# One transfer per attention unit for queries, keys and results, and a fixed order of conv taps and attention steps

## The chip, the core and the metric

The kernel runs on one core of a Trainium2 chip. The metric is the time of one execution on the device in microseconds (us), read as the median of several runs. The core has a matmul engine (TensorE, PE in the profile, with its weight loads as PEld), a vector engine (VectorE, DVE), an engine for activations and copies (ScalarE, ACT), a general engine (GpSimd, POOL) and a queue (SyncE, SP) that here issues every DMA.

## The reference

One hybrid decoder block over 2048 positions and 1024 channels, in float32. A normalized input is projected into eight sections. One branch is a gated depthwise convolution with 31 taps, a layer norm, SiLU and a gate; the other is sliding-window attention with 16 query heads, 4 key/value heads of 64 and a sink for each head. Both are projected out, merged by per-channel sigmoid gates, projected again and added to the input, and the sum is normalized.

```
h = rmsnorm(x); glu_in, conv_gate, q, k, v, attn_gate, merge = split(h @ w_in)
c = a * sigmoid(b)                    # a, b = halves of glu_in
c = silu(layernorm(depthwise_conv(c, 31 taps, causal) + b_dw))
y_conv = (c * silu(conv_gate)) @ w_conv_out
s = rope(q) . rope(k) / 8             # queries in blocks of 128, keys: own and previous block
s = where(0 <= distance < 128, s, -1e30); m = max(max(s), sink)
p = exp(s - m); probs = p / (sum(p) + exp(sink - m))
y_attn = ((probs @ v) * silu(attn_gate)) @ w_attn_out
out = rmsnorm(x + (g_conv * y_conv + g_attn * y_attn) @ w_out)
```

## The kernel before

**Precision.** Each float32 operand of a product is split into a high half (a cast) and a low half (the difference), and each product is three matmuls: high by high, low by high, high by low. Names with `whi_` and `wlo_` are the halves of a weight; `raw_` is the weight as it is loaded, in two transfers of 128 x 512 (0 and 1 at the end of a name). ScalarE casts it (L268) and GpSimd subtracts (L253). The low half is stored to `d_lo` in the first sweep (L284) and loaded from there in the second (L270).

**Sweeps and items.** The sequence is done in two sweeps of 1024 positions. In each, TensorE works through a list of items; an item is one 128-column slice of a projection over two halves of 512 positions, 16 products, each of three matmuls of 128 x 512 in a planned time of 0.68 us. The items of the projections are named ga/gb (the convolution's input), q_a/q_b, v, ag (attention gate), cg (conv gate), ma/mc (merge gates); later come ya, yc and o. TensorE's order is the program's.

**Conv taps.** VectorE does the convolution: eight groups of 128 channels, 31 taps each, one instruction of 128 x 1024 per tap (L513 for the first, L520 for the others), 248 in a sweep. The program emits one for every 2.4 us of planned time while attention runs.

**Attention.** A sweep has 32 units (4 key/value heads by 8 blocks of 128 queries), one for every 13.8 us of planned time. Queries and keys are stored to DRAM in split halves (`d_q`, L648; `d_k`), and each unit loads its own: four query transfers (L736) and four key transfers (L740) of 32 partitions each into a tile `qk`. Values are stored to `d_v`, and `load_v` (L715) brings them back for four blocks of one head in six transfers into `vm`, `va`, `vb`. A unit's steps are: scores `sc` on TensorE (L774) into two PSUM banks; ScalarE copies (L787, L789) and VectorE's masked copies (L790) into `ss`; the maximum on VectorE (L793, `st`); four exponentials on ScalarE (L795); the reciprocal (L797); four scalings on ScalarE (L799); four transposes on TensorE (L804, `tpp`); the cast on ScalarE (L813) and the split on VectorE (L253 from L814) into `pt`; two masked parts on GpSimd (L817, `pc`); the product with the values (L828, `ov`); two copies, two sums, the gate and a split (L836 to L842), and two transfers of the result to `d_a`. `sc` (twice), `tpp` and `ov` take turns on three PSUM banks, so the second bank of a unit's scores is the one that the split of the unit before sets free.

**What sets the order.** `Line` plans a time: each product adds 0.68 us to it, and a generator's step that is due is emitted between two products (`yield a, b`: TensorE time that the step costs, and how long until the next step). So steps stand in the program, and on TensorE, by planned time. On the other engines and on the queue a scheduler orders instructions by priority and planned readiness; a `Line` step and what stands in `front()` has a high priority. A conv tap may so be placed well ahead of its place in the program, or between two steps of one unit. `prepare_attention` flushes the stores of queries, loads unit 0's queries and keys, and twelve transfers of values.

## Time and profile before

| | |
|---|---|
| median of 3 runs | 2027.77 us |
| lowest and highest run | 2024.05, 2028.27 us |
| profiled execution | 2025.42 us |
| its span | 2023.7 us |
| mean granted TensorE clock | 0.995 |
| DMA packets, bytes | 302784, 382.03 MB |

One execution was profiled. Its span runs from the first to the last instruction that the page counts, 1.7 us less than the time of that execution. Times in the views are microseconds from the start of the span. In a group, `xN` is the number of instructions, followed by busy time, mean duration in ns, and the engine's idle time just before them with the instruction that ended it. In a timeline a row is start, duration, engine, line, operation, result and source, with the idle time before it in brackets. `SPq` is the queue that issues DMAs: the duration there is that of the issue, not of the transfer. Attention runs from about 197 to 690 us in the first sweep, and from about 1194 to 1684 us in the second.

### The profile page before, as it was taken

Reading aid. Unit: us, or ns where it says so; the run is one execution under the profiler, and the core shown is the slowest. Engines: PE = TensorE matmul, PEld = TensorE weight load, DVE = VectorE, ACT = ScalarE, POOL = GpSimd, SP = SyncE. Lnnn points to the kernel's source line nnn. Section 1 sums busy time; section 2 is a strip of 40 time slices with the busy share of each in tenths; the row PEclk is TensorE's granted clock in tenths of the full one; section 3 lists DMA queues with packets and bytes.
Section 4 is the critical chain, followed back from the end, with each engine's and each line's share of the span. In section 5 each row is a group of like instructions: output and inputs, shape, how many; then the busy total and the mean of one; then the engine's idle time right before and its main releaser. Section 6 shows DMA issues by size and latency. Waiting matters only on the chain.

```text
span 2023.7 us, 27913 instructions
## 1 busy us (share of the span) xinstructions
PE 1989.0 (98%) x9264; PEld 1656.4 (82%) x9264; DVE 1302.1 (64%) x1737; ACT 976.3 (48%) x2253; POOL 430.2 (21%) x462
## 2 busy tenths in 40 slices
PE   8999999999999999999999999999999999999998
PEld 7888788888888888888887887888888888888887
DVE  7999569878984275143857668579878834431424
ACT  7322576555546356244523125765565554552422
POOL 0444233333323322340011121111111110001200
PEclk9999999999999999999999999999999999999999
DMA  8655655556566855356646556665666677554532
GB/s 304 207 168 175 218 173 187 181 178 186 177 195 212 272 191 190 118 197 236 216 151 210 157 162 204 180 186 176 182 180 192 192 234 253 190 174 136 200 128 83
DMA packets 302784, 382.03 MB, mean 189 GB/s; under 512 B 30000, under 2 KB 160944, under 8 KB 302640
## 3 DMA queue, kind: packets, MB, share of 16 engines
q1 hardware_dynamic: 302640, 380.25, 58.0%
q8 instruction: 73, 1.20, 0.2%
q14 instruction: 71, 0.58, 0.1%
HBM read 252.20 MB, written 127.93 MB: 188 GB/s over the span
## 4 chain that ended last, share of the span: by engine, by line
PE 64%; DVE 16%; ACT 5%; issue 4%; DMA 1%; POOL 0%; SPq 0%; ACTq 0%; DVEq 0%; POOLq 0%
DVE acc L520 10%; PE mm_mc L291 9%; PE o L1148 9%; PE mm_ya L291 9%; PE mm_yc L291 9%; PE mm_ma L291 6%; PE mm_ag L291 5%; PE mm_ga L291 5%; PE mm_gb L291 4%; PE mm_q_a L291 2%; PE mm_q_b L291 2%; PE sc L774 1%; ACT ss L795 1%; DVE st L793 1%; PE mm_v L291 1%
## 5 line engine op out<-in xcount | busy, mean ns | idle before, releaser
L520 DVE SCALAR_TENSOR_TENSOR acc<-glu,par,acc 128x1024 f32<-128x1024 f32 x464 | 595.6, 1284 | 6.3
L1148 PE MATMUL o<-wo,mT 128*128 128x512 f32 x768 | 174.8, 389 | 0.0
L1148 PEld LDWEIGHTS o<-wo,mT 128*128 128x128 f32 x768 | 144.2, 188 | 30.0
L291 PE MATMUL mm_ag<-hT,whi_ag 128*128 128x512 f32 x512 | 161.0, 396 | 0.0
L291 PE MATMUL mm_cg<-hT,whi_cg 128*128 128x512 f32 x512 | 160.1, 394 | 0.0
L291 PE MATMUL mm_ma<-hT,whi_ma 128*128 128x512 f32 x512 | 160.0, 394 | 0.0
L795 ACT ACTIVATE ss<-ss,st 128x129 f32<-128x129 f32 x256 | 100.2, 394 | 123.9 <-DVE st L793 123.6
L291 PE MATMUL mm_mc<-hT,whi_mc 128*128 128x512 f32 x512 | 158.3, 390 | 0.0
L291 PE MATMUL mm_ya<-aT,whi_ya 128*128 128x512 f32 x512 | 157.7, 389 | 0.0
L291 PE MATMUL mm_yc<-uT,whi_yc 128*128 128x512 f32 x512 | 157.7, 389 | 0.0
L817 POOL TENSOR_SCALAR_AFFINE_SELECT pc<-pt 64x512 fp32r<-64x512 f32 x128 | 83.6, 653 | 311.1 <-ACT pt L813 268.8
L291 PE MATMUL mm_ga<-hT,whi_ga 128*128 128x512 f32 x448 | 141.4, 397 | 0.0
L291 PE MATMUL mm_gb<-hT,whi_gb 128*128 128x512 f32 x448 | 140.7, 395 | 0.6 <-DVE rb_q__1_1660 L602 0.6
L291 PEld LDWEIGHTS mm_ya<-aT,whi_ya 128*128 128x128 f32 x512 | 96.1, 188 | 20.0
L291 PEld LDWEIGHTS mm_yc<-uT,whi_yc 128*128 128x128 f32 x512 | 96.1, 188 | 19.9
L291 PEld LDWEIGHTS mm_mc<-hT,whi_mc 128*128 128x128 f32 x512 | 95.4, 188 | 19.4
L291 PEld LDWEIGHTS mm_ag<-hT,whi_ag 128*128 128x128 f32 x512 | 94.2, 190 | 17.8
L291 PEld LDWEIGHTS mm_ma<-hT,whi_ma 128*128 128x128 f32 x512 | 93.1, 188 | 17.2
L291 PEld LDWEIGHTS mm_cg<-hT,whi_cg 128*128 128x128 f32 x512 | 92.9, 188 | 17.0
L291 PE MATMUL mm_ag<-hT,wlo_ag 128*128 128x512 f32 x256 | 100.6, 393 | 3.6 <-DMA wlo_ag<-d_lo 3.6
L291 PE MATMUL mm_cg<-hT,wlo_cg 128*128 128x512 f32 x256 | 100.0, 391 | 0.0
L291 PE MATMUL mm_ma<-hT,wlo_ma 128*128 128x512 f32 x256 | 100.0, 391 | 0.0
(450 smaller groups left out, 4218.1 us busy)
## 6 DMA issues: line engine op xcount, KB each, us to landing
qk<-d_q SPq DMA_DIRECT2D x256, 64.0 KB, 2.6
d_a<-ss SPq DMA_DIRECT2D x128, 128.0 KB, 2.6
aT<-d_a SPq DMA_DIRECT2D x32, 512.0 KB, 5.3
qk<-d_k SPq DMA_DIRECT2D x240, 64.0 KB, 2.0
d_q<-hq_c SPq DMA_DIRECT2D x16, 512.0 KB, 4.2
raw_ag<-in_w_in_dram SPq DMA_DIRECT2D x32, 256.0 KB, 3.4
d_ag<-ag SPq DMA_DIRECT2D x32, 256.0 KB, 2.5
pc<-d_ag SPq DMA_DIRECT2D x64, 128.0 KB, 2.5
```

The lines of the kernel that those rows point to most:

```text
L291: pe.matmul(out=ps, lhsT=a, rhs=b, start=(k == 0 and i == 0), stop=(k == KC - 1 and i == 2))
L520: dve.scalar_tensor_tensor(out=to, in0=glu[c][:, j:j + T], scalar=tap(c, j), in1=acc[c], op0=ALU.mult, op1=ALU.add)
L774: pe.matmul(out=scs[qh][:, hp, c0:3 * HD], lhsT=w, rhs=k[:, j, qh * HD + c0:qh * HD + 3 * HD], start=(j == 0), stop=(j == 1))
L793: dve.tensor_reduce(out=ngm, in_=ext, axis=AX.X, op=ALU.max, negate=True)
L795: act.activation(out=ext[:, h, :], in_=ext[:, h, :], func=AF.Exp, bias=ngm[:, h:h + 1], accum_out=den[:, h:h + 1])
L817: pool.affine_select(out=pc[at], in_=f(pt[0:HD, a]), pattern=[[0, 2 * GQ], [1, HD]], compare_op=ALU.is_ge, fill=0.0, base=0, channel_multi ...
L1148: pe.matmul(out=ps, lhsT=a[:, c0:c0 + P], rhs=r, start=(k == 0 and i == 0), stop=(k == KC - 1 and i == 2))
```

## The change

*Layouts and transfers.* `d_q`, `d_k` and `d_a` get layouts in which a unit's data are one block: one transfer for its queries (128 x 512), one for its keys (128 x 512, or 128 x 256 in the first block), and one for its result, in place of four, four and two. Keys are stored with high and low half beside each other, in two transfers per call in place of one. Scores read the keys in pieces of 64 columns with the other half between them.

*Order.* A function `od` puts a mark "chain" on an instruction; marked ones keep the program's order among each other on their engine. It is put on the conv taps, on attention's steps on VectorE and ScalarE, and on the loads of weights, values, queries and keys. `front()` is no longer used there.

*Pieces.* The generator of a unit yields more often, so its steps are emitted in more and smaller pieces, each with its own planned time. A set `soft` is now what tells whether a unit of that head has come so far that the next head's attention gate must have been stored.

```diff
@@ -156,10 +156,10 @@
...
-    d_q = dram.tile([2, 2, P, S // HD, 2, P], F32, name="d_q")
-    d_k = dram.tile([2, 2, P, S], F32, name="d_k")
-    d_a = dram.tile([NSWEEP * KC, P, 2, T], F32, name="d_a")
+    d_q = dram.tile([P, 2, 2, S // HD, 2, P], F32, name="d_q")
+    d_k = dram.tile([P, 2, 2, S // HD, 2, HD], F32, name="d_k")
+    d_a = dram.tile([NSWEEP * NKV, P, 2, 2, T], F32, name="d_a")
     d_v = dram.tile([S // P, P, 2, NKV, P], F32, name="d_v")
...
+    def od(op):
+        tc.stamp_issue_order_token(op.ins, "chain")
+        return op
     n_w = 84
...
                 raw, hi, lo = (home[i][:, kh] for i in range(3))
-            nc.sync.dma_start(out=raw, in_=src[:, 4 * kh:4 * kh + 4, :])
+            od(nc.sync.dma_start(out=raw, in_=src[:, 4 * kh:4 * kh + 4, :]))
             act.copy(hi, raw)
             if (at, kh) in lo_stored:
-                nc.sync.dma_start(out=f(lo), in_=d_lo[at, kh])
+                od(nc.sync.dma_start(out=f(lo), in_=d_lo[at, kh]))
             else:
...
                 acc[c] = cv_ps.tile([P, T], F32, tag="acc", name=f"acc{s}_{c}")
-                dve.tensor_scalar(out=acc[c], in0=glu[c][:, 0:T], scalar1=tap(c, 0), scalar2=cbias(c),
-                                  op0=ALU.mult, op1=ALU.add)
+                od(dve.tensor_scalar(out=acc[c], in0=glu[c][:, 0:T], scalar1=tap(c, 0), scalar2=cbias(c),
+                                     op0=ALU.mult, op1=ALU.add))
...
                     to = cv[c] = slot(C[c], [P, T], F32, f"cv{s}_{c}")
-                dve.scalar_tensor_tensor(out=to, in0=glu[c][:, j:j + T], scalar=tap(c, j),
-                                         in1=acc[c], op0=ALU.mult, op1=ALU.add)
+                od(dve.scalar_tensor_tensor(out=to, in0=glu[c][:, j:j + T], scalar=tap(c, j),
+                                            in1=acc[c], op0=ALU.mult, op1=ALU.add))
                 if j == TAPS - 1:
...
         def store_k(i, half, src):
-            hl = slot(next_of("hl", AT[7:11]), [P, 2, TH], F32R, f"hlk{s}_{half}_{i}")
-            put_split(hl, src, dve)
-            t0 = s * T + half * TH
-            nc.sync.dma_start(out=d_k[:, i, :, t0:t0 + TH].rearrange("a p t -> p a t"), in_=f(hl))
+            hl = slot(next_of("hl", AT[7:11]), [P, NB, 2, HD], F32R, f"hlk{s}_{half}_{i}")
+            src = src.rearrange("p (b t) -> p b t", t=HD)
+            act.copy(hl[:, :, 0], src)
+            split_lo(hl[:, :, 1], src, hl[:, :, 0], dve)
+            b0 = 2 * s * NB + half * NB
+            for a in range(2):
+                nc.sync.dma_start(out=d_k[:, a, i, b0:b0 + NB], in_=f(hl))
...
             def load(to, rows, kind, blk):
-                nc.sync.dma_start(out=f(to), in_=d_v[blk, rows, kind, g].rearrange("b p d -> p b d"))
+                od(nc.sync.dma_start(out=f(to), in_=d_v[blk, rows, kind, g].rearrange("b p d -> p b d")))
...
             t = slot(next_of("qk", AT[11:13]), [P, 2, 4 * P], F32R, f"qk{s}_{n}")
-            q, k = t[:, 0, :].rearrange("p (b t) -> p b t", t=P), t[:, 1, :].rearrange("p (a t) -> p a t", a=2)
+            q, k = t[:, 0, :].rearrange("p (b t) -> p b t", t=P), t[:, 1, :].rearrange("p (b a t) -> p b a t", a=2, t=HD)
             qk[n] = (q, k)
             fs = slice(g * HH, (g + 1) * HH)
-            for i in range(4):
-                nc.sync.dma_start(out=f(q[i * HH:(i + 1) * HH]), in_=d_q[i // 2, i % 2, fs, 2 * blk:2 * blk + 2].rearrange("p b h t -> p (b h) t"))
-            k0 = max(blk - 1, 0) * P
-            nk = (blk + 1) * P - k0
-            for i in range(4):
-                nc.sync.dma_start(out=f(k[i * HH:(i + 1) * HH, :, 2 * P - nk:]),
-                                  in_=d_k[:, i % 2, fs, k0:k0 + nk].rearrange("a p t -> p a t"))
-        begun = set()
+            od(nc.sync.dma_start(out=f(q), in_=d_q[fs, :, :, 2 * blk:2 * blk + 2].rearrange("p a i b h t -> (p a i) (b h) t")))
+            b0 = 2 * max(blk - 1, 0)
+            nb = 2 * blk + 2 - b0
+            od(nc.sync.dma_start(out=f(k[:, 4 - nb:]), in_=d_k[fs, :, :, b0:b0 + nb].rearrange("p a i b c t -> (p a i) b c t")))
+        begun, soft = set(), set()
...
                         pe.matmul(out=scs[qh][:, hp, c0:3 * HD], lhsT=w,
-                                  rhs=k[:, j, qh * HD + c0:qh * HD + 3 * HD], start=(j == 0), stop=(j == 1))
+                                  rhs=k[:, qh + c0 // HD:qh + 3, j, :], start=(j == 0), stop=(j == 1))
...
                 pool.memset(sb, NEG)
-            with front():
-                for qh, sc in enumerate(scs):
-                    part = sb[:, 2 * qh:2 * qh + 2, :]
-                    if not first:
-                        act.copy(part, sc[:, :, 0:P])
-                    elif qh:
-                        act.copy(part[:, :, HD:], sc[:, :, HD:P])
-                    dve.copy_predicated(out=part[:, :, 0:HD], mask=tri_i, data=sc[:, :, P:3 * HD])
+            parts = [sb[:, 2 * qh:2 * qh + 2, :] for qh in range(2)]
+            for qh, part in enumerate(parts):
+                if not first:
+                    od(act.copy(part, scs[qh][:, :, 0:P]))
+                elif qh:
+                    od(act.copy(part[:, :, HD:], scs[qh][:, :, HD:P]))
+            yield 0.90, 0.8
+            for part, sc in zip(parts, scs):
+                od(dve.copy_predicated(out=part[:, :, 0:HD], mask=tri_i, data=sc[:, :, P:3 * HD]))
             st = work.tile([P, 3, GQ], F32, tag="st", name=f"st{u}", bufs=4)
             ngm, den, rinv = (st[:, i, :] for i in range(3))
-            dve.tensor_reduce(out=ngm, in_=ext, axis=AX.X, op=ALU.max, negate=True)
+            od(dve.tensor_reduce(out=ngm, in_=ext, axis=AX.X, op=ALU.max, negate=True))
+            yield 0.0, 1.2
             for h in range(GQ):
-                act.activation(out=ext[:, h, :], in_=ext[:, h, :], func=AF.Exp, bias=ngm[:, h:h + 1],
-                               accum_out=den[:, h:h + 1])
-            dve.reciprocal(out=rinv, in_=den)
+                od(act.activation(out=ext[:, h, :], in_=ext[:, h, :], func=AF.Exp, bias=ngm[:, h:h + 1],
+                                  accum_out=den[:, h:h + 1]))
+            yield 0.0, 3.3
+            od(dve.reciprocal(out=rinv, in_=den))
+            yield 0.0, 0.6
             for h in range(GQ):
-                act.activation(out=sb[:, h, :], in_=sb[:, h, :], func=AF.Copy, scale=rinv[:, h:h + 1])
-            yield 0.90, LAT[0]
+                od(act.activation(out=sb[:, h, :], in_=sb[:, h, :], func=AF.Copy, scale=rinv[:, h:h + 1]))
+            soft.add(n)
+            yield 0.0, LAT[0] - 5.9
...
             flat = tpp.rearrange("p h q -> p (h q)")
-            with front():
-                act.copy(pt[:, 0], flat)
-                split_lo(pt[:, 1], flat, pt[:, 0], dve)
+            od(act.copy(pt[:, 0], flat))
+            yield 0.44, 0.5
+            od(split_lo(pt[:, 1], flat, pt[:, 0], dve))
             for a in range(2):
...
                                    compare_op=ALU.is_ge, fill=0.0, base=0, channel_multiplier=-1)
-            yield 0.44, LAT[1]
+            yield 0.0, LAT[1] - 0.5
...
             to = [oT[own].rearrange("p i (q t) -> p i q t", t=HD) for own, _ in rows]
-            with front():
-                for r in range(2):
-                    act.copy(to[r], ovp[rows[r][1], :, r])
-                for r in range(2):
-                    dve.tensor_tensor(out=to[r], in0=ovp[rows[r][0], :, r], in1=to[r], op=ALU.add)
-            dve.tensor_tensor(out=oT, in0=oT, in1=ga, op=ALU.mult)
+            for r in range(2):
+                od(act.copy(to[r], ovp[rows[r][1], :, r]))
+            yield 0.72, 0.6
+            for r in range(2):
+                od(dve.tensor_tensor(out=to[r], in0=ovp[rows[r][0], :, r], in1=to[r], op=ALU.add))
+            od(dve.tensor_tensor(out=oT, in0=oT, in1=ga, op=ALU.mult))
+            yield 0.0, 1.6
             hl = sb.rearrange("p (l c) q -> p l c q", c=2)
-            act.copy(hl[:, 0].bitcast(F32R), oT)
-            split_lo(hl[:, 1].bitcast(F32R), oT, hl[:, 0], dve)
+            od(act.copy(hl[:, 0].bitcast(F32R), oT))
+            yield 0.0, 0.5
+            od(split_lo(hl[:, 1].bitcast(F32R), oT, hl[:, 0], dve))
             if n == NKV * NB - 1 and s + 1 < NSWEEP:
...
                     "p g (a d) -> p g a d", d=HD))
-            yield 0.72, 4.0
+            yield 0.0, 1.0
...
             def store():
-                for i in range(2):
-                    nc.sync.dma_start(out=d_a[e2, :, i, qs].rearrange("c p q -> p c q"), in_=hl[:, i])
+                nc.sync.dma_start(out=d_a[s * NKV + g, :, :, :, qs], in_=hl)
                 done[n] = True
...
                 line.after(22.0 + n * ATT_EVERY, attention(n),
-                           lambda n=n: (n > 0 or 0 in qk or 0 in begun) and (n not in begun or ("ag", 2 * (n // NB) + 1) in stored))
+                           lambda n=n: (n > 0 or 0 in qk or 0 in begun) and (n not in soft or ("ag", 2 * (n // NB) + 1) in stored))
             line.every = CONV_EVERY
...
```

Line numbers after the change are 5 to 11 higher: taps L518 and L525 for L513 and L520, masked copies L796 for L790, maximum L799 for L793, reciprocal L805 for L797, the split L258 for L253, loads L272 and L275 for L267 and L270, L723 for L715, L743 and L746 for L736 and L740.

The orders below show instructions as they stand on an engine, each with the line, the operation, the result and the source (numbers at the end of a name tell buffers apart).

VectorE, first sweep, fifth block of the second head (`ss_1_4`, with the split `pt_1_3` of the block before), and `acc`, the tap that is added. Before:

```order
L790 COPY_PREDICATED ss_1_4_3591<-tri,sc_1_4_0_3581 128x2x64
L520 SCALAR_TENSOR_TENSOR acc_4_3628<-glu_4_3225,par,acc_4_3628 128x1024
L790 COPY_PREDICATED ss_1_4_3591<-tri,sc_1_4_1_3586 128x2x64
L520 SCALAR_TENSOR_TENSOR acc_4_3628<-glu_4_3225,par,acc_4_3628 128x1024
L793 TENSOR_REDUCE st_1_4_3597<-ss_1_4_3591 128x4
L520 SCALAR_TENSOR_TENSOR acc_4_3628<-glu_4_3225,par,acc_4_3628 128x1024 x2
L797 RECIPROCAL st_1_4_3597<-st_1_4_3597 128x4
L520 SCALAR_TENSOR_TENSOR acc_4_3628<-glu_4_3225,par,acc_4_3628 128x1024
L253 TENSOR_TENSOR pt_1_3_3650<-tpp_1_3_3643,pt_1_3_3650 128x512
```

After the change, the same place:

```order
L796 COPY_PREDICATED ss_1_4_3501<-tri,sc_1_4_0_3491 128x2x64
L796 COPY_PREDICATED ss_1_4_3501<-tri,sc_1_4_1_3496 128x2x64
L799 TENSOR_REDUCE st_1_4_3517<-ss_1_4_3501 128x4
L518 TENSOR_SCALAR acc_4_3533<-glu_4_3139,par 128x1024
L525 SCALAR_TENSOR_TENSOR acc_4_3533<-glu_4_3139,par,acc_4_3533 128x1024
L805 RECIPROCAL st_1_4_3517<-st_1_4_3517 128x4
L525 SCALAR_TENSOR_TENSOR acc_4_3533<-glu_4_3139,par,acc_4_3533 128x1024
L258 TENSOR_TENSOR pt_1_3_3564<-tpp_1_3_3557,pt_1_3_3564 128x512
```

Both masked copies and the maximum now follow each other, and three taps stand ahead of the split in place of five. The first tap of group 4 (L518) stands here now, and before further up.

The queue (SP), second sweep, the weights of the second q_b item: `wlo_q_b` is the low half of its second transfer, `d_v<-vt` and `d_v<-vd` stores of values. Before:

```order
L687 DMA d_v<-vd_1_1_9893 128x4x256
L685 DMA d_v<-vt_2_9781 128x2x256
L685 DMA d_v<-vt_3_9785 128x2x256
L715 DMA vb_10726<-d_v 64x4x128 x2
L715 DMA va_10725<-d_v 64x4x128
L715 DMA vb_10726<-d_v 64x4x128
L270 DMA wlo_q_b_9823<-d_lo 128x512
```

After the change:

```order
L272 DMA raw_q_b_9605<-in_w_in_dram 128x512
L695 DMA d_v<-vd_0_1_9562 128x4x256
L693 DMA d_v<-vt_2_9565 128x2x256
L693 DMA d_v<-vt_3_9569 128x2x256
L275 DMA wlo_q_b_9607<-d_lo 128x512
L272 DMA raw_gb_10_9712<-in_w_in_dram 128x512
```

No load of values stands ahead of the weights any more, and the low half comes right behind the stores of the first pair of values.

The queue, first sweep, where attention begins: `raw_ga_20` and `raw_ga_21` are the weights of the ga item beside which the first scores stand. Before:

```order
L267 DMA raw_ga_20_1777<-in_w_in_dram 128x512
L284 DMA d_lo<-wlo_ag_01_1592 128x512
L267 DMA raw_ga_21_1783<-in_w_in_dram 128x512
L740 DMA qk_0_1745<-d_k 32x2x128 x4
L648 DMA d_q<-hq_2_0_a_1461 128x8x128
L648 DMA d_q<-hq_2_0_c_1462 128x8x128
L648 DMA d_q<-hq_2_2_a_1465 128x8x128
L736 DMA qk_0_1745<-d_q 32x512
```

After the change:

```order
L723 DMA va_1753<-d_v 64x4x128
L723 DMA vb_1754<-d_v 64x4x128
L573 DMA d_ag<-ag_0_0_1716 128x512
L656 DMA d_q<-hq_2_1_a_1505 128x8x128
L656 DMA d_q<-hq_2_1_c_1506 128x8x128
L573 DMA d_ag<-ag_0_1_1771 128x512
L272 DMA raw_ga_20_1775<-in_w_in_dram 128x512
L272 DMA raw_ga_21_1781<-in_w_in_dram 128x512
```

The two weight loads stood ahead of the first queries and keys; now they stand behind them, behind twelve loads of values and four stores.

More of the change, by code (lines that the diff above doesn't have):

```diff
@@ L252, in split_lo @@
     def split_lo(out_, full, hi, eng):
-        eng.tensor_tensor(out=out_, in0=full, in1=f(hi), op=ALU.subtract)
+        return eng.tensor_tensor(out=out_, in0=full, in1=f(hi), op=ALU.subtract)
     def load_w(src, name, home=None, steps=None):
@@ L648, in store @@
                         pend.append(lambda a=a: nc.sync.dma_start(
-                            out=d_q[a, i, :, b0:b0 + NB, r // 2, :],
+                            out=d_q[:, a, i, b0:b0 + NB, r // 2, :],
                             in_=f(pair[n][a]).rearrange("p b h t -> p b (h t)")))
@@ L939, in a_op @@
             aT[h][e] = slot(AT[8 * h + e], [P, 2, TH], F32R, f"aT{s}_{h}_{e}")
-            nc.sync.dma_start(out=f(aT[h][e]), in_=d_a[s * KC + e, :, :, h * TH:(h + 1) * TH])
+            nc.sync.dma_start(out=f(aT[h][e]), in_=d_a[s * NKV + e // 2, :, :, e % 2, h * TH:(h + 1) * TH])
         a_ops = [lambda e=e, h=h: a_op(e, h) for h in range(2) for e in range(KC)]
```

## The prediction

> **What bounds the kernel now.** I read the page's head and busy lines first, then the waits of TensorE, then the stretches around each wait, and last the timeline of the engines that end them.
>
> ```profile
> span 2023.7 us, 27913 instructions
> PE 1989.0 (98%) x9264; PEld 1656.4 (82%) x9264; DVE 1302.1 (64%) x1737; ACT 976.3 (48%) x2253; POOL 430.2 (21%) x462
> ```
>
> TensorE is busy for 1989.0 of 2023.7 us, and the change leaves it the same matmuls. So the most that can be won is TensorE's idle time, 34.7 us, and some hidden in its busy time as a slow clock. The waits view (line, releaser: us, times, longest) says where the idle time is:
>
> ```profile
> PE sc L774 <- DVE pt L253: 10.4, 13, 1.6
> PE mm_gb L291 <- ACT u_c L361: 5.5, 1, 5.5
> PE mm_q_b L291 <- DMA wlo_q_b<-d_lo: 4.4, 1, 4.4
> PE mm_ag L291 <- DMA wlo_ag<-d_lo: 3.6, 1, 3.6
> PE sc L774 <- issue: 2.9, 1, 2.9
> PEld sc L774 <- DVE pt L253: 13.3, 16, 1.8
> ```
>
> Five causes. The 5.5 us at mm_gb is the start of the program, which the change doesn't touch. The others it does: score matmuls (sc) that wait for VectorE's pt split, in 16 places by the weight loads' count; two places that wait for a weight's low half; and the first scores, which wait for queries. The view by windows (PE, PEld, DVE, ACT, POOL busy, then the granted clock, DMA share, GB/s) shows what a stop costs beside itself:
>
> ```profile
> 413.00:416.00 3.00, 3.00 (x8) 2.32 (x8) 2.92 (x5) 0.45 (x1) 1.28 (x1) 0.51 0.75 233
> 1097.70:1101.60 3.90, 3.90 (x11) 3.10 (x12) 0.00 (x0) 0.00 (x0) 0.00 (x0) 0.62 0.77 272
> 1220.20:1224.80 4.60, 4.60 (x18) 3.82 (x19) 4.40 (x6) 1.78 (x4) 0.00 (x0) 0.64 0.95 311
> ```
>
> After each of these three stops TensorE runs 3 to 4.6 us at a clock of 0.51 to 0.64: a loss of (1 − 0.51) × 3.00 = 1.5 us after 412, (1 − 0.62) × 3.90 = 1.5 at 1097, 1.7 at 1220.
>
> The stop at 412 stands for the 16. VectorE, ScalarE and TensorE, in this order:
>
> ```profile
> 404.19 0.30 DVE L790 COPY_PREDICATED ss<-tri,sc 128x128 f32<-128x128 int32 x1
> 404.38 1.28 DVE L520 SCALAR_TENSOR_TENSOR acc<-glu,par,acc 128x1024 f32<-128x1024 f32 x1
> 405.57 0.30 DVE L790 COPY_PREDICATED ss<-tri,sc 128x128 f32<-128x128 int32 x1
> 405.77 1.28 DVE L520 SCALAR_TENSOR_TENSOR acc<-glu,par,acc 128x1024 f32<-128x1024 f32 x1
> 406.96 0.68 DVE L793 TENSOR_REDUCE st<-ss 128x4 f32<-128x516 f32 x1
> 407.56 2.60 DVE L520 SCALAR_TENSOR_TENSOR acc<-glu,par,acc 128x1024 f32<-128x1024 f32 x2
> 411.40 0.68 DVE L253 TENSOR_TENSOR pt<-tpp,pt 128x512 fp32r<-128x512 f32 x1
> 407.74 0.40 ACT L795 ACTIVATE ss<-ss,st 128x129 f32<-128x129 f32 x1 [4.72 <-DVE st L793]
> 409.30 0.56 ACT L813 CAST pt<-tpp 128x512 fp32r<-128x512 f32 x1
> 402.56 0.60 PE L804 MATMUL tpp<-ident_r,ss 128*128 128x128 f32 x4
> 409.91 0.58 PE L774 MATMUL sc<-qk 128*128 128x192 f32 x4
> 412.14 0.83 PE L774 MATMUL sc<-qk 128*128 128x192 f32 x4 [1.65 <-DVE pt L253]
> ```
>
> The transposed probabilities (tpp) are ready at 403.2, and their bank is needed again by the next scores at about 410.5. Between lie the ScalarE cast, which stands behind four exponentials, which wait (4.72 us) for the reduction, which stands behind two taps of 1.28 us; and then the split, which stands behind three more taps. VectorE isn't idle anywhere in between, but 6.4 us of what it does there are taps (1.28 each, with one more at 410.20) that nobody waits for: its order sets the stop, not its load.
>
> **The change, part by part.** *VectorE's and ScalarE's order.* In the change both mask copies and the reduction stand together, then come three taps, the reciprocal among them, and the pt split. From the durations above: copies and reduction 404.19 + 2 × 0.30 + 0.68 = 405.5, so the exponentials begin 407.74 − 405.5 = 2.2 us earlier, and the cast with them, at 409.30 − 2.2 = 407.1. The split comes after three taps instead of five, at 405.5 + 3 × 1.28 + 0.2 = 409.5 instead of 411.40, and ends at 410.2, ahead of the need at 410.5. Against it, tpp is emitted one to two steps of 0.68 us later, as each new piece of the generator rounds up to a step; the split isn't tied to tpp (403.2) but to its queue, so this costs slack and no wait. I take all of the 13.3 us as gained, with the 1.5 us of slow clock after 412, and put 1.2 us back for places where 0.3 us of margin is not enough. Bounds: if all of the 16 waits return at half their length, the gain is 6.7; if they return in full, nothing; it can't exceed 14.8.
>
> The cover of that: taps now keep their place in the program, and no longer run ahead. Before, VectorE did all of them by here:
>
> ```profile
> 616.78 1.27 DVE L520 SCALAR_TENSOR_TENSOR cv<-glu,par,acc 128x1024 f32<-128x1024 f32 x1
> 421.00:620.00 199.00, 196.88 (x987) 165.75 (x986) 167.66 (x227) 109.42 (x317) 69.08 (x82) 1.00 0.59 183
> 620.00:690.00 70.00, 69.86 (x343) 58.65 (x342) 19.34 (x40) 35.37 (x98) 22.80 (x26) 1.00 0.77 251
> ```
>
> By the order of the change the last tap stands beside the last unit, which TensorE reaches near 690. With taps spread until then, VectorE's load over the whole stretch is (167.66 + 19.34) / 269 = 70% in place of 84% and then 28%. The same work fits, and the queue in front of each attention step gets shorter. What is used up is a cover of some 70 us between the last tap and the convolution's normalization; some microseconds of it stay, and I cost that at nothing. If it is gone, TensorE waits for the excess, up to 5 us a sweep.
>
> *Second sweep, weights of q_b.* Before, value loads (L715) stood ahead of the second low half:
>
> ```profile
> 1093.72 0.61 SPq L715 DMA_DIRECT2D vb<-d_v  x1
> 1094.43 0.55 SPq L270 DMA_DIRECT2D wlo_q_b<-d_lo  x1
> 1097.69 0.50 PE L291 MATMUL mm_q_b<-hT,wlo_q_b 128*128 128x512 f32 x1 [4.37 <-DMA wlo_q_b<-d_lo]
> ```
>
> Twelve value loads are issued between the two halves of q_b's weights. In the change none is: they wait for the attention's preparation. Twelve issues at 0.61 are 7.3 us, more than the wait of 4.4. So −4.4, and −1.5 of slow clock behind it. Bounds: −5.9 to 0, since the value stores still stand in between.
>
> *Where the twelve went.* They now stand in one block behind unit 0's query and key loads, ahead of the next item's weights, in both sweeps.
>
> ```profile
> 200.44 3.20 SPq L736 DMA_DIRECT2D qk<-d_q  x5
> 206.08 0.52 SPq L568 DMA_DIRECT2D d_ag<-ag  x1
> L715 SPq DMA_DIRECT2D va<-d_v x32: 573/612/1292, 81.0 to 1589.7; - x32
> raw_ga<-in_w_in_dram SPq DMA_DIRECT2D x30, 256.0 KB, 3.3
> 409.77 0.62 ACT L268 CAST whi_ga<-raw_ga 128x512 fp32r<-128x512 f32 x1
> 203.74 2.54 POOL L253 TENSOR_TENSOR wlo_ga<-raw_ga,whi_ga 128x512 fp32r<-128x512 f32 x2
> 208.16 0.39 PE L291 MATMUL mm_ga<-hT,wlo_ga 128*128 128x512 f32 x1
> 211.49 1.94 PE L774 MATMUL sc<-qk 128*128 128x64 f32 x8 [2.94 <-issue]
> ```
>
> First sweep: the change issues queries and keys from 200.4 (two issues, 1.0), twelve value loads (7.3) and four stores (2.1), and only then raw_ga of the item that TensorE reaches at 207.7: issue at 210.8, landing 3.3 later at 214.1, the cast 0.6, the split 1.3, so 216.0. Before, these weights were issued ahead of the queries, and TensorE stopped for 2.94 for the queries, which now come first. TensorE has its 0.5 us of high-half matmuls and 0.9 us of scores before it needs the low half: 216.0 − 207.7 − 1.4 = 6.9 in place of 2.94, so +4.0. Bounds: +1 (issues at their shortest, and the cover of ready work larger than I count) and +8 (the query load waits another 3.4 us for the landing of the store just ahead of it).
>
> Second sweep, the wait at 1220:
>
> ```profile
> 1209.56 5.07 SPq L736 DMA_DIRECT2D qk<-d_q  x6
> 1215.82 1.98 SPq L270 DMA_DIRECT2D wlo_ag<-d_lo  x2
> 1220.17 0.50 PE L291 MATMUL mm_ag<-hT,wlo_ag 128*128 128x512 f32 x1 [3.61 <-DMA wlo_ag<-d_lo]
> ```
>
> In the change the stores of queries come first, then one query and one key load (1.0), the twelve value loads (7.3) and the weights. The six query issues of 5.07 us go out, and the wait for stores ahead of them shrinks, as the load stands behind all stores at once; if it is released at 1206 (an estimate, 3.5 us ahead of 1209.56), the low half is issued at 1206 + 1.0 + 7.3 + 0.5 (the raw half ahead of it) = 1214.8 in place of 1215.82. I take −0.9; bounds −3.6 (the wait gone) to +3 (released as before).
>
> *The merged transfers.* A unit issues three query loads, three key loads and one store less, 64 × 7 = 448 DMAs, and eight key stores come in. TensorE waits for queries and keys nowhere but at 211.49, and that is counted. The score matmuls read keys in pieces of 64; I take this at nothing, since the trace has no row of a strided kind; bounds 0 and, at 10% of 512 matmuls of 0.58 / 4 us, +7.4.
>
> [...] After 1.65 us of idleness at 412 the window from 413.00 shows 0.51. [...]
>
> **The sum**, on the profiled execution's 2025.4 us: −13.3 − 1.5 + 1.2 (scores) − 5.9 (q_b) + 4.0 (first weights behind value loads) − 0.9 (1220) = −16.4, so 2009.0. That execution lies 2.35 under the median of the runs, 2027.77. On the median's footing the forecast is **2011** us.
>
> **The rivals.** (1) *The waits move.* Shorter queues on VectorE are met by the steps emitted later, and scores go on waiting for the split or for the next bank's release; −13.3 − 1.5 + 1.2 shrinks to nothing, and −5.9 + 4.0 − 0.9 = −2.8 is left: 2025. For it: 0.3 us of margin in the one place worked out. Against: two taps less in the queue and the earlier cast act at every unit.
>
> (2) *Value loads hold up the weights.* The bounds on the wrong side together on SP: +8 at the first sweep, +3 at the second, and again wherever the six value loads of a later reload now keep a fixed place ahead of weights (6 × 0.61 = 3.7 us, six times a sweep, hidden while weights are early by more). With a quarter of the twelve places uncovered, +11, and the gain at the scores kept: −13.6 − 5.9 + 8 + 3 + 11 = +2.5, so 2030, slower within what can be told. It decides from the point where weights are less than 3.7 us ahead of TensorE. For it: both weight waits in this trace come from such a queue. Against: elsewhere no weight wait shows at all.
>
> (3) *Fixed order makes VectorE stand.* The program spaces units by 13.8 us, and in the stretch 421 to 620 VectorE is busy for 0.84 × 13.8 = 11.6 of them. In program order it can't fill a wait for ScalarE's exponentials (1.6 us from 407.74 to 409.30) with a tap further down. Above 2.2 us of such waits a unit it falls behind, the split is late at every unit, and at an average of 0.8 us (half the longest wait shown) over the 62 later units TensorE loses 50 us: 2027.77 + 50 − 13.3 + 10 of clock is some 2070. For it: VectorE now has no freedom at all. Against: its load falls to 70% here, 4.1 us free a unit, and the exponentials' wait has a tap or two placed in front.
>
> (4) *It doesn't do what it says:* the merged query load waits for stores of both halves and no load becomes earlier. Then the first scores lose what (2) counts, at most 3.4 us; it is inside the ranges.
>
> **How the numbers follow.** The forecast gets 0.66, with its own range 2002 to 2019 (upper end: half of the 13.3 back, +6.7, and some of the other upper bounds; lower: the first weights at +1 and the 1220 wait gone, −3.0 − 2.7, and no margin lost, −1.2). Rival 1 0.15 (2020 to 2027), rival 2 0.10 (2024 to 2036), rival 3 0.09 (2040 to 2070). Two tenths of a per cent, 4 us, is about what a measurement of this kernel can tell from no change. Faster, under 2023.7: all of the forecast and two thirds of rival 1, 0.76. Same: the rest of rival 1 and half of rival 2, 0.10. Slower: the other half of rival 2 and rival 3, 0.14. The range from 2001 to 2028 leaves out rival 3, half of rival 2 and a few hundredths below: 0.17.
>
> **What would show each step.** The order of VectorE: the row of sc waiting for pt gone or under 2 us, and the wait in front of the exponentials, 4.72 us at 407.74, shorter. The loads: no row for wlo_q_b; one for raw or wlo of ga at 208, of 5 to 9 us, with a clock near 0.5 behind it; wlo_ag at 1220 about 2.7. Taps until about 690. The forecast is wrong if sc waits stay over 7 us, if weight waits come up at more than the two places, or if VectorE shows idle time ended by ScalarE's exponentials at every unit together with late splits.

## The result and the profile after

The changed kernel takes 2012.26 us in the median of its runs (2010.38 to 2015.85), beside 2027.38 for the kernel before: a ratio of 0.9931 with a 95% interval of 0.9916 to 0.9946. A second comparison later, on the chip of the last experiments, gave 0.9935 (0.9922 to 0.9947). So it is faster by 13 to 14 us by the ratios, 15 by the first medians; 16.4 were forecast. The execution that was profiled is the slowest of the four, 2015.85, and so 3.6 us above the median, while that of the kernel before (2025.42) lay 2.0 below its own. So the two spans differ by 9.6 us only (2023.7 and 2014.1), where the medians differ by 15.1.

The head and the busy line of the page after, and TensorE's waits in full (line, releaser: us, times, longest):

```profile
span 2014.1 us, 27138 instructions
PE 1985.5 (99%) x9264; PEld 1654.0 (82%) x9264; DVE 1310.3 (65%) x1737; ACT 982.1 (49%) x2250; POOL 429.1 (21%) x462
PE mm_ga L296 <- ACT whi_ga L273: 9.6, 1, 9.6
PE mm_gb L296 <- ACT u_c L366: 5.6, 1, 5.6
PE mm_mc L296 <- ACT mc L568: 3.5, 2, 1.8
PE mm_ag L296 <- ACT whi_ag L273: 2.7, 1, 2.7
PE mm_mc L296 <- ACT rstd L935: 0.4, 1, 0.4
```

No row is left for scores that wait for the pt split (10.4 before, 13.3 by the weight loads), none for q_b's low half (4.4) and none for the first queries (2.9). In their place stands one wait of 9.6 us for the weights of ga, where 6.9 were forecast. The wait for ag is 2.7, the figure that was forecast, but it is another wait: before, TensorE stood at 1220 for a low half; now it stands from 1210.6 to 1213.3 for the high half, whose load is issued at 1209.26, right behind the twelve value loads of the second sweep (1201.36 to 1209.2). The waits at mm_mc are new.

```profile
1209.26 0.60 SPq L272 DMA_DIRECT2D raw_ag<-in_w_in_dram  x1
```

The same round of attention as in the prediction, in the timeline after, by time; it begins with the scores whose masked copies came at 404.19 before:

```profile
401.89 1.03 PE L779 MATMUL sc<-qk 128*128 128x192 f32 x8
402.51 0.82 ACT L791 COPY ss<-sc 128x256 f32<-128x256 f32 x2 [1.55 <-PE sc L779]
404.01 0.49 DVE L796 COPY_PREDICATED ss<-tri,sc 128x128 f32<-128x128 int32 x2
404.60 0.69 DVE L799 TENSOR_REDUCE st<-ss 128x4 f32<-128x516 f32 x1
405.21 2.60 DVE L525 SCALAR_TENSOR_TENSOR acc<-glu,par,acc 128x1024 f32<-128x1024 f32 x2
405.39 0.41 ACT L802 ACTIVATE ss<-ss,st 128x129 f32<-128x129 f32 x1 [1.75 <-DVE st L799]
409.60 0.60 PE L814 MATMUL tpp<-ident_r,ss 128*128 128x128 f32 x4
410.24 0.59 ACT L822 CAST pt<-tpp 128x512 fp32r<-128x512 f32 x1 [0.72 <-PE tpp L814]
410.86 0.69 DVE L258 TENSOR_TENSOR pt<-tpp,pt 128x512 fp32r<-128x512 f32 x1 [1.72 <-ACT pt L822]
415.58 1.03 PE L779 MATMUL sc<-qk 128*128 128x192 f32 x8
```

and the beginning of that round in the timeline of before:

```profile
395.63 0.59 PE L774 MATMUL sc<-qk 128*128 128x192 f32 x4
401.89 0.64 ACT L787 COPY ss<-sc 128x256 f32<-128x256 f32 x2
```

Before, ScalarE's copies came 6.3 us after the scores and VectorE's 8.6; now they come 0.6 and 2.1 after. Reduction and exponentials are over by 407 and, when the transposes come at 409.60, ScalarE casts at once and VectorE, which now waits for the cast (1.72), splits. The split ends at 411.6, 2 us after the transposes began where it took 9.5, and the next scores come at 415.6: 4 us of margin where there were −1.65. And the last tap of the sweep ends at 685.5 in place of 618.1, so VectorE's load is even:

```profile
421.00:620.00 199.00, 199.00 (x1000) 167.91 (x999) 159.77 (x219) 114.56 (x321) 70.81 (x85) 1.00 0.58 191
620.00:690.00 70.00, 70.00 (x346) 58.95 (x346) 52.05 (x67) 31.88 (x86) 22.31 (x23) 1.00 0.72 229
```

TensorE is busy for every one of these 269 us.

The new wait, in the timeline after of SP, ScalarE, GpSimd and TensorE:

```profile
199.71 0.58 SPq L743 DMA_DIRECT2D qk<-d_q  x1
200.90 1.27 SPq L723 DMA_DIRECT2D vm<-d_v  x2
208.14 0.61 SPq L723 DMA_DIRECT2D vb<-d_v  x1
212.14 1.67 SPq L272 DMA_DIRECT2D raw_ga<-in_w_in_dram  x2
217.30 0.62 ACT L273 CAST whi_ga<-raw_ga 128x512 fp32r<-128x512 f32 x1 [8.33 <-DMA raw_ga<-in_w_in_dram]
218.00 2.50 POOL L258 TENSOR_TENSOR wlo_ga<-raw_ga,whi_ga 128x512 fp32r<-128x512 f32 x2 [19.17 <-ACT whi_ga L273]
218.50:222.00 3.50, 3.37 (x12) 2.54 (x11) 0.30 (x1) 0.59 (x3) 2.00 (x2) 0.50 1.03 396
222.00:226.00 4.00, 4.00 (x11) 3.07 (x10) 3.49 (x4) 3.97 (x12) 2.53 (x2) 0.50 1.00 327
```

Twelve value loads take the queue from 200.90 to 208.75, four stores until 212.1, and only then is raw_ga issued. It lands after some 5.2 us, not the 3.3 of the prediction's row; from 212.1 to 217.3 the DMA engines' share is 1.05, but that this is why it takes longer wasn't tested. The two windows behind the wait, 7.5 us at half clock (0.50), cost another 3.7 us.

### The profile page after: what moved, and what is told of

It is laid out like the page before. It is cut to its first block, busy times and chain, and to the rows that moved or that the text cites. A ratio compares the mean times of both kernels' runs of the same rounds, so it can differ in the third digit from the quotient of the medians.

```text
span 2014.1 us, 27138 instructions
## 1 busy us (share of the span) xinstructions
PE 1985.5 (99%) x9264; PEld 1654.0 (82%) x9264; DVE 1310.3 (65%) x1737; ACT 982.1 (49%) x2250; POOL 429.1 (21%) x462
## 4 chain that ended last, share of the span: by engine, by line
PE 94%; DMA 3%; SPq 1%; DVE 1%; ACT 1%; issue 0%; POOL 0%; ACTq 0%; POOLq 0%
PE mm_ag L296 9%; PE mm_cg L296 9%; PE mm_ma L296 9%; PE o L1159 9%; PE mm_ya L296 9%; PE mm_yc L296 9%; PE mm_ga L296 7%; PE mm_gb L296 7%; PE mm_mc L296 7%; PE mm_q_a L296 4%; PE mm_q_b L296 4%; PE sc L779 3%; PE ov L838 2%; PE mm_v L296 2%; PE tpp L814 1%; PE mm_ka L296 1%
## 5 line engine op out<-in xcount | busy, mean ns | idle before, releaser
L525 DVE SCALAR_TENSOR_TENSOR acc<-glu,par,acc 128x1024 f32<-128x1024 f32 x464 | 595.6, 1284 | 7.5
L258 DVE TENSOR_TENSOR pt<-tpp,pt 128x512 fp32r<-128x512 f32 x64 | 44.2, 690 | 99.8 <-ACT pt L822 99.7
L296 PEld LDWEIGHTS mm_ga<-hT,whi_ga 128*128 128x128 f32 x448 | 83.3, 191 | 26.0 <-ACT whi_ga L273 10.1
L1041 DVE TENSOR_TENSOR lmc<-mm_yc,lmc 128x512 f32<-128x512 f32 x32 | 22.0, 688 | 126.1 <-PE mm_yc L296 126.1
```

The lines of the kernel that those rows point to most:

```text
L258: return eng.tensor_tensor(out=out_, in0=full, in1=f(hi), op=ALU.subtract)
L296: pe.matmul(out=ps, lhsT=a, rhs=b, start=(k == 0 and i == 0), stop=(k == KC - 1 and i == 2))
L525: od(dve.scalar_tensor_tensor(out=to, in0=glu[c][:, j:j + T], scalar=tap(c, j), in1=acc[c], op0=ALU.mult, op1=ALU.add))
L1041: dve.tensor_tensor(out=g, in0=ps, in1=g, op=ALU.mult)
```

## The experiments

Each was timed in five rounds beside the kernel before. Its ratio is given with the 95% interval; differences in us are ratios times 2027.5.

Two theories were set against each other. Theory A: the time comes from the order on VectorE and ScalarE, and from where the value loads stand. Theory B: it comes from fewer transfers.

### The merged transfers alone

```diff
  (before.py with the new layouts)
+ one query, key and result transfer per unit; rhs=k[:, qh + c0 // HD:qh + 3, j, :]
  (no mark, front() and the long pieces as before)
```

> The kernel before with the merged transfers alone (new layouts, one query, key and result transfer per unit, strided keys in the scores); order and pieces as before. Theory A (the time comes from the order on VectorE and ScalarE, and from where value loads stand): the scores still wait for the pt split 10 to 15 us in all, q_b's low half is waited for by 4 to 5 us, and the time is within 4 us of the kernel before. Theory B (fewer transfers on the queue bring it): scores wait under 4 us, and at least 8 of the 15 us are gained.

Measured: 2018.64 us, 0.9955 (0.9943 to 0.9968), 9.1 us under the kernel before.

```profile
PE sc L774 <- DVE pt L253: 13.3, 16, 1.7
PE mm_q_b L291 <- DMA wlo_q_b<-d_lo: 4.7, 1, 4.7
```

Neither expectation holds in full: the waits are those of theory A, and yet 9.1 of the 14 us are there, more than the 8 of theory B. The rows that are gone tell why: the wait of 2.9 for the first queries and that of 3.6 for ag's low half, with the slow clock behind both (before, 0.50 from 211.5 to 218 and 0.64 from 1220.2 to 1224.8; the mean granted clock of the profiled execution is 0.998 here and 0.995 before). The queue reaches the first scores' queries and ag's weights earlier, since it has fewer issues ahead: ag's first low half is issued at 1203.94, where it was 1215.82. Two waits, not a general relief, for the sum closes: 6.5 us of waits gone, 4.2 less of TensorE's busy time (1989.0 to 1984.8; the matmuls are the same), and 3.2 more at the split and q_b make 7.5 of the 7.8 us between the spans.

### The order without the merged transfers

```diff
  (after.py with the layouts of before)
- od(nc.sync.dma_start(out=f(q), ...))
+ for i in range(4): od(nc.sync.dma_start(out=f(q[i * HH:(i + 1) * HH]), ...))   # keys too; two for the result
```

> The changed kernel with the transfers and layouts of before (four query, four key and two result transfers a unit), its order and pieces kept. Theory A: the wait for the pt split stays under 2 us, q_b waits for nothing, the first ga weights are waited for by 9 to 14 us since more issues stand ahead of them, and the time is 0 to 6 us above the changed kernel. Theory B: within 5 us of the kernel before.

Measured: 2017.13 us, 0.9953 (0.994 to 0.9967), as theory A has it.

```profile
PE mm_ga L296 <- ACT whi_ga L273: 12.1, 1, 12.1
PE mm_ag L296 <- ACT whi_ag L273: 6.3, 1, 6.3
PE sc L779 <- DVE pt L258: 0.3, 1, 0.3
```

The split waits are gone (0.3) without any merged transfer. What the merge gives inside the changed kernel is 4.5 us by the ratios, whose intervals overlap; by the waits it is 2.5 us at ga and 3.6 at ag. ga's weights are issued at 213.97 here and at 212.14 in the changed kernel: issues that stand ahead of the weights count.

### Taps free to run ahead

```diff
- od(dve.scalar_tensor_tensor(out=to, in0=glu[c][:, j:j + T], ...))   # and the first tap
+ dve.scalar_tensor_tensor(out=to, in0=glu[c][:, j:j + T], ...)
```

> The changed kernel with the mark taken off the conv taps, so that they may again run ahead of their place; the attention steps and the loads keep it. Theory A (it is the taps between a unit's steps that made the split late): five or six taps stand ahead of the split in many units, the scores wait for it 7 us or more, and the time is 6 to 14 us above the changed kernel. Rival: the smaller pieces and the fixed order of the attention steps alone do it; the wait stays under 3 us and the time within 3 us of the changed kernel.

Measured: 2042.87 us, 1.0074 (1.0062 to 1.0087): slower than the kernel before by 15 us and than the changed kernel by 29.

```profile
PE sc L779 <- DVE pt L258: 16.0, 18, 2.1
PE mm_ga L296 <- ACT whi_ga L273: 11.5, 1, 11.5
PE mm_ag L296 <- DMA raw_ag<-in_w_in_dram: 6.2, 1, 6.2
```

Without the mark on the taps, the rest of the change is a loss. It is twice the loss expected: the split waits come back in full, the two weight waits are 1.9 and 3.5 us longer, and the waits for mm_mc L568 (3.5) are gone. These sum to 18 of the 23.7 us between the two spans; the rest is slow clock (a mean of 0.992 here and of 0.994 in the changed kernel: 0.008 × 2038 − 0.006 × 2014 = 4 us) and scattered. Theory A's cause holds, at twice its size; why the weight waits grew is open.

### Loads free

```diff
- od(nc.sync.dma_start(out=raw, in_=src[:, 4 * kh:4 * kh + 4, :]))    # low halves, values, queries, keys too
+ nc.sync.dma_start(out=raw, in_=src[:, 4 * kh:4 * kh + 4, :])
```

> The changed kernel with the mark taken off the loads of weights, values, queries and keys; their order is again the scheduler's. Theory A, with the moved value loads as a gain at q_b and a loss at the first ga weights: the split wait stays gone, q_b's low half is waited for by 4 to 5 us again, ga's weights by under 4 in place of 9.6, and the sum is within 4 us of the changed kernel. If the marked loads were a plain gain, it is 5 us or more slower than the changed kernel; if a plain loss, 8 us or more faster.

Measured: 1999.03 us, 0.9862 (0.9848 to 0.9875): 14 us faster than the changed kernel. It is the last of the expected cases, the marked loads as a plain loss.

```profile
PE mm_gb L296 <- ACT u_c L366: 5.8, 1, 5.8
PE mm_q_b L296 <- DMA wlo_q_b<-d_lo: 4.8, 1, 4.8
PE mm_v L296 <- DMA wlo_v<-d_lo: 0.8, 1, 0.8
PE mm_mc L296 <- ACT mc L568: 0.5, 1, 0.5
```

q_b waits again, 4.8, as said. But ga waits not by "under 4" but not at all, and ag neither: the merged transfers had already removed the two waits of before, so that the marks on the loads don't move a wait, they make one of 9.6 and one of 2.7 with half clock behind each (0.50 from 218.5 to 226 and from 1213.6 to 1217.5 in the changed kernel).

### Which loads

```diff
  (after.py) weights unmarked, values, queries and keys marked
```

> The changed kernel with the mark taken off the weight loads alone (raw and low halves); value, query and key loads, taps and steps keep it. Theory A (the marked loads lose 13 us net because weights stand behind twelve value loads, and gain 6 us at q_b because those loads left it): both gains are kept, no weight is waited for by more than 1.5 us, the time is 1989 to 1996. Rival: the marks on the value, query and key loads cost by themselves, by loads that come late; the time is 1999 or more, and scores or value products show waits for a transfer.

Measured: 2000.24 us, 0.9866 (0.9852 to 0.9879). q_b's wait is gone, but theory A's time isn't reached:

```profile
PE mm_ag L296 <- DMA wlo_ag<-d_lo: 2.6, 1, 2.6
PE mm_ag L296 <- ACT whi_ag L273: 2.3, 1, 2.3
PE mm_ag L296 <- POOL wlo_ag L258: 0.6, 1, 0.6
```

The time is the rival's, the waits are not: it is weights again that wait, in the item after ga and in ag of the second sweep. In the queue ag's low halves are issued at 1197.76, behind twelve value loads that end at 1196.5. Taking the mark off a weight doesn't by itself put it ahead of marked value loads; the scheduler placed only ga's weights there.

The next run keeps every mark and moves only the value loads:

```diff
  (after.py, all marks kept; prepare_attention)
- for n in range(2):
-     load_v(n)
- return
- yield
+ yield 0.0, 9.0
+ load_v(0)
+ yield 0.0, 12.0
+ load_v(1)
+ yield 0.0, 0.0
```

> The changed kernel, all marks kept, with the first twelve value loads emitted in two groups, 9 and 21 us of planned time behind the first query load, so that the weights of the next item stand ahead of them. Theory A: the wait for ga's weights falls from 9.6 to 0 to 4 us, that for ag's from 2.7 to under 1, and the time is 1997 to 2004. If the queue were held up by something else than the value loads, the waits stay above 7 and the time above 2008.

Measured: 1997.91 us, 0.9858 (0.9843 to 0.9873).

```profile
PE mm_ga L296 <- ACT whi_ga L273: 1.5, 1, 1.5
PE mm_mc L296 <- ACT mc L568: 0.8, 2, 0.4
PE mm_mc L296 <- ACT rstd L936: 0.7, 1, 0.7
PE mm_ga L296 <- DMA vm<-d_v: 0.6, 1, 0.6
```

Theory A holds: 2.1 us at ga in all, no row for ag. This settles where the loss comes from: with every mark in place, and only the value loads moved behind the weights, 15 us come back. The time is that of the free loads (0.9858 beside 0.9862), so fixed order on the queue costs nothing that shows here; the twelve loads at that place do.

### The pieces and the marks, apart

```diff
- tc.stamp_issue_order_token(op.ins, "chain")     # no mark at all, small pieces kept
```

> The changed kernel without any mark: merged transfers and the smaller pieces are kept, and every order but TensorE's is the scheduler's. Theory A (the taps have to be held): up to eight taps stand ahead of a split, scores wait for it 10 us or more, and the time is 2018 to 2040. Rival (the smaller pieces bring the gain, the marks nothing): split waits under 4 us and 1996 to 2004.

Measured: 2026.31 us, 0.9997 (0.9988 to 1.0006): no different from the kernel before, and as theory A has it.

```profile
PE sc L778 <- DVE pt L257: 15.2, 14, 2.9
```

```diff
  (marks on taps and steps, loads free) a unit's generator in three pieces:
- yield 0.90, 0.8 ... yield 0.0, 1.2 ... yield 0.0, 3.3 ... yield 0.0, 0.6 ... yield 0.0, LAT[0] - 5.9
+ yield 0.90, LAT[0]
  (0.44, LAT[1] and 0.72, 4.0 as before)
```

> The changed kernel with the mark on taps and attention steps alone, and a unit's generator in the long pieces of before. Theory of the fixed order that makes an engine stand: in long pieces the reciprocal stands right behind the reduction, VectorE is idle 2 us or more before each of the 64 reciprocals, the tap sequence falls behind, and the time is 2010 to 2060. Rival (only the place of the taps counts): idle time before reciprocals as without marks, 64 us in all, and a time within 4 us of 1999, where the same marks in small pieces stand.

Measured: 2010.71 us, 0.992 (0.9906 to 0.9933), at the lower end of the theory's range.

```profile
PE sc L779 <- DVE pt L258: 7.8, 7, 2.0
```

These two make a square with the merged transfers alone and the loads free, all with merged transfers and unmarked loads (the first cell has the raised priority of `front()` in place of the marks; ratio to the kernel before, and TensorE's wait for the split):

| | no mark on taps and steps | marks |
|---|---|---|
| long pieces | 0.9955, 13.3 us | 0.9920, 7.8 us |
| small pieces | 0.9997, 15.2 us | 0.9862, 0 |

The marks gain 7 us in long pieces (against `front()`) and 27 in small ones (against neither). The small pieces gain 12 with marks. In the first column the lower cell is 8.5 us slower, but it lacks `front()` too, so how much of that is the pieces' isn't shown. VectorE's waits for the exponentials, of the two kernels with marks, long pieces first:

```profile
DVE st L802 <- ACT ss L800: 146.8, 64, 3.6
DVE st L805 <- ACT ss L802: 11.7, 21, 1.0
```

In long pieces the reciprocal stands right behind the reduction and VectorE stands 2.3 us at each of the 64 units; in small ones taps lie between and it waits 0.2. Without marks the same wait is 63.9 us at 28 units (the merged transfers alone). That is the first half of the prediction's third rival, VectorE standing at every unit; its second half, a late split at every unit, doesn't follow even here: the split is waited for at 7 units.

### A version that keeps what works

```diff
  (the deferred value loads, and)
- line.after(10.0, prepare_attention(), lambda: True)
+ line.after(13.0, prepare_attention(), lambda: True)
```

> The kernel with the deferred value loads, and the preparation of attention 13 instead of 10 us of planned time after its start, so that the weights of the next ga item stand ahead of the first query load too. Theory A: the remaining wait for ga's weights (1.5 and 0.6 us, with 1.5 us of slow clock behind) goes, the first scores may wait up to 2 us for the query load, and the time is 1993 to 1999, 13 to 18 us under the changed kernel. If the first scores wait 3 us or more, it is no better than the deferred loads alone.

> The changed kernel once more, on the chip of this comparison. 2009 to 2016 us, with a wait for ga's weights of 9 to 11 us and one for ag's of 2 to 4.

Measured: 1993.35 us (1992.13 to 1995.87), 0.9831 (0.9818 to 0.9845), 34 us under the kernel before; the changed kernel beside it 2015.31, 0.9935 (0.9922 to 0.9947), with a wait of 10.2 us for ga's weights and one of 2.9 for ag's. The gain over the changed kernel is 21 us by the ratios, where 13 to 18 were expected. TensorE's waits in this version:

```profile
PE mm_gb L296 <- ACT u_c L366: 5.5, 1, 5.5
PE mm_mc L296 <- ACT rstd L936: 1.0, 1, 1.0
PE mm_mc L296 <- ACT mc L568: 0.5, 1, 0.5
190.00:230.00 40.00, 40.00 (x186) 33.37 (x185) 19.48 (x25) 21.16 (x48) 17.29 (x19) 1.00 1.00 315
```

From 190 to 230, where the kernel before and the changed one stop, TensorE is busy throughout at full clock (1.00). The first scores don't wait for their queries either. Of TensorE's waits, the start and 1.5 us are left.

## Why the prediction was right in its sum, and not in its parts

**The sum** was −16.4; the ratios give −14. By edit it came about otherwise. The measured column goes in one order (merge alone, then marks and pieces on VectorE and ScalarE, then marks on the loads); another order would divide the sum otherwise, since in the changed kernel the merge is worth 4.5 us and not 9.1:

| edit | forecast | measured |
|---|---|---|
| merged transfers | −2.9 inside "where the twelve went", else nothing | −9.1 |
| order on VectorE and ScalarE | −13.6 | −18.9 |
| marks on the loads | −5.9 + 6.9 − 0.9 = +0.1 | +14.0 |
| sum | −16.4 | −14.0 |

**VectorE's and ScalarE's order: right place, another size.** The waits for the split are gone. The 1.2 us that I put back for a lack of margin didn't come: at the place worked out, the margin is 4 us and not 0.3. The step that failed there is the count "after three taps instead of five" from 404.19: I moved the split against the masked copies and took the copies to stay where they were. What moved most is the copies themselves, from 8.6 to 2.1 us behind their scores; beside the five taps that I saw between the steps I had missed those ahead of the first. That the split is tied to its queue and not to the transposes doesn't hold after the change either: VectorE is there early and waits 1.72 us for the cast, which waits for them. The edit's gain of 18.9 also passes my bound of 14.8. With merged transfers the edit removes 13.3 us of TensorE's waits for the split and another 6.6 of its busy time (1984.8 to 1978.2), where I had counted 1.5 us of slow clock behind one of the 16 waits. The mean granted clock, 0.998 with the merged transfers alone and 0.999 with the loads free, accounts for about 2 us of the 6.6 (0.002 × 2016 − 0.001 × 1997); where the rest comes from wasn't shown.

**The merged transfers: the failed step is the price of nothing.** I counted TensorE's one wait for queries, and credited the wait at 1220 to the order of loads. The merge alone removes both with their slow clock (a mean of 0.998 for 0.995). The fourth rival, a merged load that is no earlier, is out with it: in that run the first scores run at 208.35 without a wait. The 2.7 us at ag in the changed kernel were met by luck. I had the queue let go at 1206 and the low half issued at 1214.8; it let go at 1200.51 and issued it at 1209.96, TensorE came about 6 us earlier too, and what it waits for is the high half.

**Where the twelve went: right in place, wrong in size.** The term +4.0 (6.9 for 2.94) measured +6.7 (9.6 for 2.94), because the issue came at 212.14 and not 210.8 and the transfer took 5.2 us for 3.3. The wait also ends with the high half's cast, not with the low half's split as I had it; by my own figures that would have been 7.0 us (214.1 + 0.6 − 207.7), so this changed little. That the clock would stay at half behind it I had taken as unchanged from before. The granted clock is 0.50 from the end of the stop, 217.97, to 226.1, 8.1 us, where it was 0.50 for some 6.5 before (211.49 to 218); with the loads free and the transfers merged there is no such wait, and the mean clock is 0.999 for 0.994. The second rival, value loads that hold up weights, was a part of what happened; it did not show at the later reloads, where I had priced it at +11.

**q_b: right.** No wait is left in the changed kernel; free loads bring back 4.8 us.

**The cover of the taps: right as far as shown.** The last tap ends at 685.5, and the split sums that open the normalization begin at the same time as before, 688.70 for 688.64. The 3.5 us at mm_mc come later: copies of mc stand on ScalarE behind squares that wait, once 2.51 us for a transfer of mc. With the loads free 0.5 is left, with marked loads in a better place 0.8, and with the taps free none. So neither the marks on the taps nor those on the loads make it alone; what starts it is open.

**The strided keys** cost nothing that shows: scores that don't wait run 1.03 us for 8 matmuls with them (457.37) as without (455.20 in the kernel before).

**The range.** Its lower end, 2002, is 2 us below what its own terms give (2011 − 6.9 = 2004); the result doesn't turn on it.

The third rival was wrong for the change as made and half right for its coarser form.

The errors had opposite signs, +14 on the loads and −11.5 on the two others. That they cancel is luck: the sum was met, while single parts were off by up to 14 us.

## What to carry over

Fix the order of long filler work (here the taps) as well as that of the short chain that it fills in: with the chain and the loads fixed and the taps free, this kernel was 15 us slower than before. The taps alone weren't tried. An order fixed by program text is only as good as the text: cut the chain where one engine waits for another, and emit bulk loads behind the weights that are needed first. Price each edit by what it does alone and with the others, since two waits at one place, removed by either edit, are counted once.

## What was not expected of the hardware

Stops of TensorE of nearly the same length had different clocks behind them. In the kernel before, a stop of 1.65 us ends at 412.14, and the clock granted over the next 8 us is 0.79 (0.51 from 413 to 416); one of 1.60 us ends at 1547.05, and it is 1.00. In the changed kernel it is 1.00 behind stops of 1.77 us, which ends at 727.70, and of 1.73 us, which ends at 1711.82. The four stretches of 8 us, in this order:

```profile
412.14:420.14 8.00, 8.00 (x33) 6.59 (x33) 7.89 (x11) 2.24 (x6) 1.93 (x3) 0.79 0.75 225
1547.05:1555.05 8.00, 8.00 (x39) 6.74 (x40) 2.90 (x7) 6.88 (x16) 2.66 (x3) 1.00 0.75 237
727.70:735.70 8.00, 8.00 (x35) 6.65 (x36) 1.57 (x3) 3.20 (x6) 2.65 (x2) 1.00 0.67 228
1711.82:1719.82 8.00, 8.00 (x35) 6.65 (x36) 1.57 (x3) 3.23 (x6) 0.00 (x0) 1.00 0.82 261
```

What makes the difference wasn't shown. The first row costs (1 − 0.79) × 8 = 1.7 us beside the stop, the other three nothing more. So my estimate from these rows prices a stop of 1.60 to 1.77 us in this kernel at itself plus nothing or 1.7 us.
